# Three more row units in seven products, two of them worked in pairs; a norm's root as a power; another order in the last unit

## The chip, the cores and the metric

The kernel runs on one core of a Trainium2 chip. The metric is device time in microseconds (us), the median of three runs. Beside it stands one execution that the hardware profiler recorded; its views are what is quoted below. In them PE is TensorE's matmul, PEld its weight load, DVE is VectorE, ACT is ScalarE, POOL is GpSimd and SP is SyncE, which issues most DMAs. "L705" is a line of the kernel's source.

## The reference

One layer of a streaming encoder in fp32 on x of 1024 positions by 1024 channels; the feed-forward width is 3072:

```python
h = rms_norm(x, norm1_w)
q, k, v, g_ret, x_lru, y_lru, gate_ret, gate_lru = split(h @ w_in)       # 1024 x 7168
q, k = rotary(q), rotary(k) * dk**-0.5
o = chunkwise_retention(q, k, v)                   # 4 heads, chunks of 64
y_a = (head_group_norm(o, ret_gn_w) * silu(g_ret)) @ w_ret_o
hl = rg_lru(causal_conv(x_lru), ...)               # block-diagonal gates, scan over positions
y_b = (hl * gelu(y_lru)) @ w_lru_o
mix = sigmoid(gate_ret + b0) * y_a + sigmoid(gate_lru + b1) * y_b
x = x + mix @ w_out
h = rms_norm(x, norm2_w)
gate, val = split(h @ ffn_w_up)                    # 1024 x 6144
x = x + (gelu(causal_conv3(gate)) * val) @ ffn_w_down     # 3072 x 1024
return rms_norm(x, norm_f_w)
```

## The kernel before, in words

**Units.** Every large product is cut into *units* (class `Job`): a block of 256 output rows (two 128-row halves m) by 1024 positions (two 512-column halves) with 1024 inner channels (two halves k). The operand with the positions, four blocks B11, B12, B21, B22 of four 128x512 tiles each, stays in SBUF for all units of a product; the weights A11, A12, A21, A22 of each unit are loaded from DRAM. For fp32 accuracy each tile is split in a high and a low part (`split`: ACT casts at L424, DVE subtracts at L425), and each product of a weight tile with an operand tile is three matmuls 128x128 by 128x512 (`PASSES`).

**Eight or seven products.** One block product is 4 tiles x 3 passes = 12 matmuls. A *standard* unit makes 8 of them, 96 matmuls (`mm_std`, `mm_by` at L650, `mm_first` L681). A *fast* unit uses the scheme of Strassen and Winograd with 7, so 84 matmuls (`mm_fast`, L705). It takes sums of weight blocks (S1 = A21+A22, S2 = S1-A11, S3 = A21-A11, S4 = A12-S2, made by DVE at L510 to L526) against sums of operand blocks (T1 = B12-B11, T2 = B22-T1, T3 = B12-B22, T4 = B21-T2). Products and sets go together so: A11 with B11, S1 with T1, S2 with T2, A12 with B21, S3 with T3, A22 with T4, S4 with B22, in this order. The results gather in three PSUM banks X, Y and Z; ACT copies a bank out (`keep`, L719), DVE adds (`more` L725, `total` L729). The operand sets are made once for all units of a product by *builders* (`operand` loads blocks and splits them, `tsets` makes T1 to T4 tile by tile).

Standard before are the four units of the retention output, the first of LRU output, of FFN up and of FFN down, and the very first unit of all (the constants `FAST_RO`, `FAST_LO`, `STD_U` and `g + t` say which are fast).

**The order of the work.** The kernel body is Python that emits instructions while generators for weight loads (`loads`, L470), weight preparation (`preps`) and builders are advanced between products. It is built twice: class `Plan` reads the instructions of the first build with their dependencies, gives each a due time in a backward pass with costs set by hand, and lists them in a forward pass (`forward`): on each engine the most urgent ready instruction is next. The second build is held to that order on every engine, SP's queue of DMAs included.

**Places that the steps below speak of.** At the start `params` (128 rows of 200 columns of scales and biases) comes by one DMA on ACT's queue (L1462), the first x tile beside it (L1458); DVE then scales x tiles into high and low parts (L878 to L881, ACT's part of it at L880 and L893). The rotary turn swaps two halves of a tile by DMAs (L1175, L1176), multiplies and adds on DVE (L1177 to L1179) and transposes on PE (L1187). Gates are written to DRAM as they are finished (`sg_d`, L1305). After the output product the second RMSNorm turns positions into columns: statistics (L1547, L1548), root (`rstd_of`, L796 to L801, on ACT and DVE), scaling (L1569), PE transposes (L1577), evictions as high part, low part and plain copy (L1580 to L1582); L1115 is a PE product of the LRU gates. FFN down sums its parts in `down_sums`, the last unit ends with the final norm (squares at L1742, a power on POOL at L1746, scaling at L1753, output DMA).

Of the kernel before, what the change touches and what calls it, by code (L numbers as in the profile page):

```python
# [18 lines left out]
P = 128  # L19
D = 1024  # L20
T = 1024
KT = 8
# [176 lines left out]
class Plan:  # L199
# [6 lines left out]
    LATE_DMA, LATE_PE, BACKLOG, KEEP = 1500.0, 400.0, 300.0, 2000.0  # L206

# [12 lines left out]
    def __init__(self, steps, nc):  # L220
        self.steps = {s.name: s for s in steps if s.outs and s.eng in self.ENGINES}
        edges = {n: [a for a, _ in nc.dependency_edges(n, None)] for n in nc.inst_names()}
        self.before, self.after = {}, {n: [] for n in self.steps}
        for n in self.steps:
            found, todo, seen = [], [n], {n}
            while todo:
                for a in edges.get(todo.pop(), ()):
                    if a not in seen:
                        seen.add(a)
                        (found if a in self.steps else todo).append(a)  # L230
            self.before[n] = found
            for a in found:
                self.after[a].append(n)
# [60 lines left out]
    def forward(self, rank):  # L294
# [16 lines left out]
        for _ in range(len(self.steps)):  # L311
# [13 lines left out]
            if e == "Activation" and switch(item[1]) and item[0] > t + self.KEEP:  # L325
                item = min((q for q in ready[e] if not switch(q[1])), default=item)
            ready[e].remove(item)
# [6 lines left out]
            order[e].append(n)  # L334
            free[e] = t + s.hold
# [29 lines left out]
PASSES = ((0, 0), (0, 1), (1, 0))  # L365
NU = 81
# [18 lines left out]
def tile_trunk_layer(ctx, tc, x, xt, positions, params, consts, normf, w_in, w_ro, w_lo,  # L385
# [51 lines left out]
    class Job:  # L437
        def __init__(self, src, op, emit, post=None, fast=False, last=False, drop12=False,
                     pre=None, fetch=None, order=None, ready=None, by=None, rate=RATE):
            self.pre, self.ready, self.by, self.rate = pre, ready, by, rate  # L440
            self.order = order or (("A11", "A21", "A22", "A12") if fast else ORD_T)
# [17 lines left out]
    def loads():  # L459
        i = 0  # L460
        while True:
            while i >= len(queue):
                yield None
            jb = queue[i]
            for nm in jb.order:
                m, kh = int(nm[1]) - 1, int(nm[2]) - 1
                while jb.ready is not None and not jb.ready(m, kh):
                    yield None
                t = W.get()
                SY.dma_start(t, jb.src(m, kh))  # L470
                jb.raw[nm] = t
                state["raws"] += 1
                yield True
            i += 1
# [11 lines left out]

    def preps():
        i = 0
        while True:
            while i >= len(queue):  # L490
                yield None
            jb = queue[i]

            def fin(nm, src):
                jb.blk[nm] = split(src, W.get)
                state["blocks"] += 1

            if not jb.fast:
                for nm in jb.order:
                    fin(nm, (yield from raw(jb, nm)))  # L500
                    done(jb, nm)
                    yield True
            else:
                a11 = yield from raw(jb, "A11")
                fin("A11", a11)
                yield True
                a21 = yield from raw(jb, "A21")
                a22 = yield from raw(jb, "A22")
                s1 = W.get()
                V.tensor_add(s1, a21, a22)  # L510
                fin("S1", s1)
                yield True
                V.tensor_sub(s1, s1, a11)  # L513
                fin("S2", s1)
                yield True
                a12 = yield from raw(jb, "A12")
                fin("A12", a12)
                yield True
                V.tensor_sub(a11, a21, a11)  # L519
                fin("S3", a11)  # L520
                done(jb, "A11", "A21")
                yield True
                fin("A22", a22)
                done(jb, "A22")
                yield True
                V.tensor_sub(s1, a12, s1)  # L526
                fin("S4", s1)
                W.put(s1, late=SOONER)
                done(jb, "A12")
                yield True  # L530
            i += 1
# [163 lines left out]
    def mm_fast(jb, op):  # L695
        X, Y, Z = psg.get(), psg.get(), psg.get()

        def prod(bank, an, bn, first):
            pump((jb, an))
            w = jb.blk[an]  # L700
            n = 0
            for j in range(4):
                c = slice(128 * j, 128 * j + 128)
                for a, b in PASSES:
                    PE.matmul(bank, w[a][:, c], need(op, (bn, j))[b], start=first and n == 0, stop=n == 11,  # L705
# [4 lines left out]
            if jb.last:  # L710
                for j in range(4):
                    drop(op.pop((bn, j)))
            pump()
            build(BRATE)
            advance(RATE)

        def keep(bank):
            u = get()
            S.copy(u, bank)  # L719
            return u  # L720

        def more(u, m, c):
# [4 lines left out]

        def total(u, bank, m, c):
            V.tensor_add(u, bank, u)  # L729
            jb.emit(m, c, u, u)  # L730

        prod(X, "A11", "B11", True)
        s1 = keep(X)
        yield
        jb.ask(0, 0)
        prod(Z, "S1", "T1", True)
        prod(X, "S2", "T2", False)
        u2 = keep(X)
        more(s1, 0, 0)
        jb.ask(1, 1)  # L740
        prod(Y, "A12", "B21", True)
        total(s1, Y, 0, 0)
        psg.put(Y)
        jb.ask(1, 0)
        prod(X, "S3", "T3", False)
        u3 = keep(X)
        more(u3, 1, 1)
        total(u3, Z, 1, 1)
        yield
        jb.ask(0, 1)  # L750
        prod(X, "A22", "T4", False)
        jb.emit(1, 0, X, None)
        psg.put(X)
        more(u2, 0, 1)
        prod(Z, "S4", "B22", False)
        total(u2, Z, 0, 1)
        psg.put(Z)

    def run(jobs, between=None):
# [4 lines left out]
        ahead = None  # L764
        for jb, nx in zip(jobs, jobs[1:] + [None]):
            if jb.fast:
                g = ahead
                if g is None:
                    g = mm_fast(jb, jb.op)
# [3 lines left out]
                if nx is not None and nx.fast and nx.op is jb.op:  # L773
                    ahead = mm_fast(nx, nx.op)
# [8 lines left out]
            if jb.post is not None:  # L783
                g = jb.post()
                if g is not None:
                    back.append(g)
# [46 lines left out]
    def tsets(op, fetch, ahead=AHEAD_T, here=False):  # L833
        tiles = reads(fetch, [(n, j) for j in range(4) for n in ("B11", "B12", "B21", "B22")], ahead)
        for j in range(4):
# [16 lines left out]
            yield 2.4  # L852

# [579 lines left out]
    def u_start():  # L1433
        drain()
        builders.append(operand(u, from_dram(u_d), FAST_LO > 0))
# [11 lines left out]
    half = pool.tile([P, 1], F32, tag="half", name="half")  # L1447
# [14 lines left out]
    nc.scalar.dma_start(par, params)  # L1462
# [8 lines left out]
    for k in (2, 3):  # L1471
        xget(k, 0)
    next(state["load"])
# [70 lines left out]
    def out_post(t):  # L1544
        def fn():
# [3 lines left out]
            rstd_of(r, v, w)  # L1549
# [4 lines left out]
    def norm_half(half):  # L1554
# [18 lines left out]
        for k in range(KT):  # L1573
# [5 lines left out]
            hi, lo, f = get(F32R), get(F32R), get()  # L1579
            S.activation(hi, ps, AF.Copy, scale=w)  # L1580
            V.scalar_tensor_tensor(lo, ps, w, hi.bitcast(F32), ALU.mult, ALU.subtract)
            S.activation(f, ps, AF.Copy, scale=w)  # L1582
            h2[f"B{k // 4 + 1}{half + 1}", k % 4] = (hi, lo)
            keep2[f"B{k // 4 + 1}{half + 1}", k % 4] = f
# [261 lines left out]
```

## Time and profile before

| | before |
|---|---|
| median of three runs | 1614.21 us (1613.81 to 1616.84) |
| profiled execution, its own time | 1613.97 us |
| span of that execution | 1612.2 us |
| PE busy | 1599.3 us, 99% of the span |
| DVE, ACT, POOL busy | 1320.6 (82%), 908.2 (56%), 45.8 (3%) |
| matmul records of fast units (L705), of `mm_by` (L650) | 5544, 768 |
| DMA | 271.11 MB, 168 GB/s in the mean |

The span is what the records cover; the execution's own time is 1.8 us longer. Busy times are sums of the records of one engine; those of PE overlap, so its share says that it hardly stops, and the price of one matmul is read from a chain of many in a row. Where another engine or a DMA matters, it does so only at the few places at which PE waits.

### The profile page before, as it was taken

The page shows a single profiled execution, that of the slowest core. Times are in us where ns is not written, and L with a number is a line of the kernel's source. Part 1 is how long each engine was busy: PE and PEld are TensorE (multiplying, and loading weights), DVE is VectorE, ACT ScalarE, POOL GpSimd, SP SyncE. Part 2 cuts the span into 40 slices and gives each one's busy share as a digit, 9 for nine tenths or more (in the row PEclk, how much of TensorE's full clock was granted, in tenths as well). Part 3 has the DMA queues.
Part 4 walks back from the last instruction along what each step waited for, and adds up shares of the span by engine and source line. Part 5 has one row for each costly group of instructions (what it writes and reads, how often), then busy time and mean ns, then how long its engine had stood idle before and what let it go on. Part 6 is the DMA issues. An engine that isn't in the chain of part 4 may idle for free.

```text
span 1612.2 us, 21662 instructions
## 1 busy us (share of the span) xinstructions
PE 1599.3 (99%) x7176; PEld 1320.5 (82%) x7176; DVE 1320.6 (82%) x2393; ACT 908.2 (56%) x1534; POOL 45.8 (3%) x68
## 2 busy tenths in 40 slices
PE   9999999999999999999999999999999999999998
PEld 7887888888888888888888888888888888888886
DVE  8998768686898899968788799777777778888885
ACT  7475535444696878934364775444444446554553
POOL 0010000000000000000000001000000000000000
PEclk9999999999999999999999999999999999999999
DMA  8245324242242337775797236444444456878761
GB/s 298 66 133 162 118 72 138 66 131 85 92 144 95 128 93 267 236 261 201 228 333 248 99 124 199 142 131 137 137 133 144 135 189 217 285 241 277 256 217 66
DMA packets 151441, 271.11 MB, mean 168 GB/s; under 512 B 16800, under 2 KB 25120, under 8 KB 151328
## 3 DMA queue, kind: packets, MB, share of 16 engines
q1 hardware_dynamic: 145664, 253.63, 48.3%
q0 software_dynamic: 4224, 13.64, 2.7%
q10 hardware_dynamic: 1440, 2.46, 0.4%
q8 instruction: 56, 0.92, 0.2%
q14 instruction: 57, 0.47, 0.1%
HBM read 188.92 MB, written 75.50 MB: 164 GB/s over the span
## 4 chain that ended last, share of the span: by engine, by line
PE 61%; DVE 2%; ACT 2%; issue 1%; POOLq 0%; POOL 0%; DVEq 0%; ACTq 0%
PE g L705 50%; PE g L650 10%; DVE u L1097 1%; PE a L1115 1%; DVE u L425 0%; PE a L1577 0%; ACT u L1118 0%; DVE w L425 0%; ACT L1118 0%; ACT L1138 0%; DVE u L729 0%; ACT u L424 0%; ACT u L1126 0%; DVE u L1058 0%; ACT L1304 0%
## 5 line engine op out<-in xcount | busy, mean ns | idle before, releaser
L705 PE MATMUL g<-u,w 128*128 128x512 f32 x5544 | 1296.1, 392 | 0.7 <-ACT u L719 0.7
L705 PEld LDWEIGHTS g<-u,w 128*128 128x128 f32 x5544 | 1035.3, 188 | 212.2 <-ACT u L719 1.1
L424 ACT CAST w<-w 128x512 fp32r<-128x512 f32 x502 | 309.8, 621 | 405.0 <-PE g L705 280.6
L425 DVE TENSOR_TENSOR w<-w,w 128x512 fp32r<-128x512 f32 x502 | 342.0, 685 | 91.0 <-ACT w L424 86.8
L729 DVE TENSOR_TENSOR u<-g,u 128x512 f32<-128x512 f32 x198 | 135.7, 687 | 78.3 <-PE g L705 58.9
L650 PE MATMUL g<-u,w 128*128 128x512 f32 x768 | 179.6, 390 | 0.0
L424 ACT CAST u<-u 128x512 fp32r<-128x512 f32 x224 | 132.0, 620 | 70.4 <-PE g L705 12.4
L650 PEld LDWEIGHTS g<-u,w 128*128 128x128 f32 x768 | 143.7, 188 | 29.4
L719 ACT COPY u<-g 128x512 f32<-128x512 f32 x198 | 114.9, 580 | 76.4 <-PE g L705 74.9
L425 DVE TENSOR_TENSOR u<-u,u 128x512 fp32r<-128x512 f32 x224 | 146.5, 684 | 4.8 <-ACT u L424 4.5
L1623 DVE SCALAR_TENSOR_TENSOR u<-u,par,u 128x511 f32<-128x511 f32 (+1 forms) x96 | 71.4, 745 | 3.9 <-ACT u L1620 3.5
L1628 POOL DMA_DIRECT2D ff_d<-u x48 | 36.1, 752 | 1237.6 <-DVE u L1627 1237.6
L1115 PE MATMUL a<-u,u 128*128 128x512 f32 x192 | 50.4, 394 | 0.6 <-ACT u L424 0.4
L1620 ACT ACTIVATE u<-u,par 128x512 f32<-128x512 f32 x48 | 39.3, 818 | 15.4 <-DVE u L729 15.0
L513 DVE TENSOR_TENSOR w<-w,w 128x512 f32<-128x512 f32 x66 | 45.3, 687 | 1.2
L519 DVE TENSOR_TENSOR w<-w,w 128x512 f32<-128x512 f32 x66 | 45.3, 686 | 0.5
L526 DVE TENSOR_TENSOR w<-w,w 128x512 f32<-128x512 f32 x66 | 45.3, 686 | 0.4
L510 DVE TENSOR_TENSOR w<-w,w 128x512 f32<-128x512 f32 x66 | 45.2, 685 | 0.5 <-DMA w<-w_up 0.4
L725 DVE TENSOR_TENSOR u<-u,u 128x512 f32<-128x512 f32 x42 | 28.8, 687 | 19.9 <-ACT u L719 19.8
L1115 PEld LDWEIGHTS a<-u,u 128*128 128x128 f32 x192 | 35.2, 188 | 10.4 <-ACT u L424 1.8
L1627 DVE TENSOR_TENSOR u<-u,u 128x512 f32<-128x512 f32 x48 | 33.0, 687 | 5.8 <-ACT u L1626 5.7
L1097 DVE SCALAR_TENSOR_TENSOR u<-u,par,u 128x511 f32<-128x511 f32 (+2 forms) x48 | 35.4, 744 | 0.0
(189 smaller groups left out, 1123.4 us busy)
## 6 DMA issues: line engine op xcount, KB each, us to landing
w<-w_in SPq DMA_DIRECT2D x112, 256.0 KB, 2.7
w<-w_up SPq DMA_DIRECT2D x96, 256.0 KB, 2.7
u<-w_dn SPq DMA_DIRECT2D x88, 256.0 KB, 3.2
u<-x_d SPq DMA_DIRECT2D x60, 256.0 KB, 4.6
x_d<-u SPq DMA_DIRECT2D x48, 256.0 KB, 3.7
ff_d<-u POOLq DMA_DIRECT2D x48, 256.0 KB, 2.9
td_d<-u SPq DMA_DIRECT2D x48, 256.0 KB, 3.1
w<-ff_d SPq DMA_DIRECT2D x48, 256.0 KB, 3.7
```

The lines of the kernel that those rows point to most:

```text
L424: S.copy(hi, src)
L425: V.tensor_sub(lo, src, hi.bitcast(F32))
L513: V.tensor_sub(s1, s1, a11)
L519: V.tensor_sub(a11, a21, a11)
L526: V.tensor_sub(s1, a12, s1)
L650: PE.matmul(banks[m, h], jb.blk[an][a][:, c], o[b], start=left[m, h] == 2 and n == 0, stop=left[m, h] == 1 and n == 11)
L705: PE.matmul(bank, w[a][:, c], need(op, (bn, j))[b], start=first and n == 0, stop=n == 11, skip_group_check=True)
L719: S.copy(u, bank)
L729: V.tensor_add(u, bank, u)
L1097: V.scalar_tensor_tensor(c[:, s:], src[:, :TH - s], w, c[:, s:], ALU.mult, ALU.add)
L1115: PE.matmul(ps, wg[g][a][:, cs], xs[k][b], start=q == 0, stop=q == 5)
L1623: V.scalar_tensor_tensor(c[:, s:], src[:, :TH - s], w, c[:, s:], ALU.mult, ALU.add)
```

## The change

**More units in seven products.** The first unit of LRU output, of FFN up and of FFN down become fast, so only the first unit of all and the four of the retention output stay standard. To have enough PE work for each operand set while the sets are still being made, the first two units of LRU output and of FFN up are worked as a pair (`mate`): product by product, first for the one, then for the other unit, with six banks; loads and weight preparation alternate likewise.

**Order of products.** A fast unit may now have its own order (`prods`): the two first FFN-up units take `EARLY` (A11, A12, S4, S1, S2, S3, A22: the plain blocks B11, B21, B22 first, the T sets after), the last FFN-down unit takes `ENDING` (A12 later and S2 ahead of S1). Two new builders make sets in the order in which products take them: `seven` for the LRU operand and the first FFN-down group (four loads of each block instead of eight), `set_by_set` for FFN up.

```diff
+PRODS = ("A11", "S1", "S2", "A12", "S3", "A22", "S4")
+ENDING = ("A11", "S2", "S1", "S3", "A12", "A22", "S4")
+EARLY = ("A11", "A12", "S4", "S1", "S2", "S3", "A22")
+SETS = {"A11": "B11", "S1": "T1", "S2": "T2", "A12": "B21", "S3": "T3", "A22": "T4", "S4": "B22"}
+BANKS = {"A11": "X", "S1": "Z", "S2": "X", "A12": "Y", "S3": "X", "A22": "X", "S4": "Z"}
...
-    def mm_fast(jb, op):
-        X, Y, Z = psg.get(), psg.get(), psg.get()
+    def mm_fast(group, op):
...
+        for i, nm in enumerate(plan):
+            for jb in group:
...
+                prod(jb, bank, nm)
+                if nm in ("A11", "S2", "S3") or over and nm == "S4":
+                    u = kept[jb, nm] = get()
+                    S.copy(u, bank)
...
+    def set_by_set(op, b):
+        for j in range(4):
+            V.tensor_sub(b["B11", j], b["B12", j], b["B11", j])
+            op["T1", j] = split(b["B11", j])
+            yield 1.2
...
     def u_start():
         drain()
-        builders.append(operand(u, from_dram(u_d), FAST_LO > 0))
+        builders.append(seven(u, from_dram(u_d)))
...
-        ojobs.append(Job(pair_src(w_lo, n), u, emit_lru_o(n), fast=n >= 4 - FAST_LO, last=n == 3,
-                        drop12=n == 3 - FAST_LO, fetch=from_sg_t1(n),
-                         by=None if n >= 4 - FAST_LO else "k", order=None if n >= 4 - FAST_LO else BY_K))
+        ojobs.append(Job(pair_src(w_lo, n), u, emit_lru_o(n), fast=True, last=n == 3, mate=n == 0,
+                         fetch=from_sg_t1(n)))
...
-        if not g:
-            yield from operand(dop[g], fetch, False)
-            yield from kept_sums(dop[g], td_d[g])
-            return
...
+    ups = [Job(pair_src(w_up, i), h2, emit_to(gvs[i % 2]), up_post(i), fast=True, last=i == NF - 1,
+               mate=i == 0, prods=EARLY if i < 2 else PRODS,
+               order=("A11", "A12", "A21", "A22") if i < 2 else None) for i in range(NF)]
...
-                 emit_down(g, t, g + t > 0), down_post(g, t), fast=g + t > 0, last=t == 3, drop12=g + t == 0,
+                 emit_down(g, t, True), down_post(g, t), fast=True, last=t == 3,
+                 prods=ENDING if (g, t) == (2, 3) else PRODS,
                  pre=((0, 0), (0, 1), (1, 1)), fetch=from_x1(t),
-                 by=None if g + t else "k", order=None if g + t else BY_K,
```

**Second norm.** The root is one power on POOL, for two columns at a time. For the second half of the positions the transposed tiles come in the order 4 to 7, then 0 to 3, and B12, which no product takes as it stands, is no longer split. **Parameters** come as 8 columns first and the other 192 after four x tiles, on SP's queue.

```diff
-            rstd_of(r, v, w)
+            G.tensor_tensor(r, v, half, ALU.pow)
...
-        for k in range(KT):
+        for k in (range(KT), (4, 5, 6, 7, 0, 1, 2, 3))[half]:
...
-            builders.append(tsets(h2, lambda n, j: keep2[n, j], here=True))
+            builders.append(set_by_set(h2, keep2))
...
-    nc.scalar.dma_start(par, params)
+    nc.scalar.dma_start(par[:, 0:8], params[:, 0:8])
...
     for k in (2, 3):
         xget(k, 0)
+    SY.dma_start(par[:, 8:], params[:, 8:])
```

**The planner.** `Plan` now also counts who freed the buffer that a later instruction of the same tile writes, and in the forward pass DVE and ACT may stay idle for an instruction that will be ready within `NEAR` after the present one would end and is due more than `APART` (10,000 ns) earlier.

```diff
+    NEAR, APART = 500.0, 10000.0
...
+            if e in ("DVE", "Activation"):
+                soon = min(((rank[n], at) for at, n in wait[e] if at < t + self.steps[item[1]].hold + self.NEAR),
+                           default=None)
+                if soon and soon[0] < min(t, item[0] - self.APART):
+                    free[e] = soon[1]
+                    continue
```

What it does to the order of the instructions is shown at three places. The first is ACT's queue at the start, before; `par` is the tile of parameters, `w_27` and `w_30` are the high parts of the first two weight tiles, the `u` tiles are x and its scaled parts:

```order
L1458 DMA u_82_95<-xt 128x512
L1462 DMA par<-params 128x200
L1466 ACT_TABLE_LOAD
L1466 ACTIVATE st<-st 128x1
L893 ACTIVATE u_146_334<-u_82_95,par 128x512
L424 CAST w_27_151<-w_23_92 128x512
L424 CAST w_30_155<-w_24_99 128x512
L880 ACTIVATE u_100_159<-u_83_97,par 128x512
```

and now:

```order
L1577 DMA u_82_95<-xt 128x512
L1581 DMA par<-params 128x8
L1585 ACT_TABLE_LOAD
L1585 ACTIVATE st<-st 128x1
L451 CAST w_27_152<-w_23_92 128x512
L451 CAST w_30_156<-w_24_99 128x512
L1000 ACTIVATE u_100_160<-u_83_97,par 128x512
```

The scaling for the sums (L893) has moved behind both casts, and the load ahead of them is 8 columns wide. The second place is SP's queue at the second rotary turn, before. The DMAs from L1175 and L1176 swap halves of a tile, `sg_d` and `y_d` are finished gates written to DRAM, `w_in` is a weight load; `u_301` and `u_247` are the same buffer under two names:

```order
L1176 DMA u_308_1542<-u_298_1385 64x512
L1175 DMA u_308_1542<-u_298_1385 64x512
L1305 DMA sg_d<-u_247_821 128x512
L1176 DMA u_301_1471<-u_293_1267 64x512
L470 DMA w_250_1430<-w_in 128x512
L1305 DMA sg_d<-u_273_1036 128x512
L1073 DMA y_d<-u_279_1172 128x512
L1176 DMA u_306_1518<-u_300_1432 64x512
L1175 DMA u_306_1518<-u_300_1432 64x512
```

and now:

```order
L1296 DMA u_308_1543<-u_298_1386 64x512
L1295 DMA u_308_1543<-u_298_1386 64x512
L1425 DMA sg_d<-u_247_820 128x512
L1425 DMA sg_d<-u_273_1037 128x512
L500 DMA w_251_1433<-w_in 128x512
L500 DMA w_250_1429<-w_in 128x512
L1296 DMA u_306_1519<-u_300_1431 64x512
L1295 DMA u_306_1519<-u_300_1431 64x512
L1193 DMA y_d<-u_294_1287 128x512
L1193 DMA y_d<-u_279_1172 128x512
L1296 DMA u_301_1471<-u_293_1266 64x512
```

The swap into `u_301`, which must wait until `u_247` is written out, stood ahead of the swap into `u_306` and stands behind it now. The third place is PE's queue in the first FFN-up units, before. `g_268`, `g_267` and `g_271` are PSUM banks, the `w` tiles are weights:

```order
L650 MATMUL g_268_8981<-u_1682_8915,w_1442_8618 128x512
L650 MATMUL g_268_8981<-u_1683_8916,w_1442_8618 128x512
L650 MATMUL g_268_8981<-u_1682_8915,w_1443_8619 128x512
L705 MATMUL g_271_9095<-u_1593_8629,w_1448_8664 128x512
L650 MATMUL g_267_8957<-u_1685_8926,w_1436_8587 128x512
L650 MATMUL g_268_8981<-u_1685_8926,w_1442_8618 128x512
L705 MATMUL g_271_9095<-u_1594_8630,w_1448_8664 128x512
```

and now, where `g_267` and `g_268` are the Z banks of the first and the second unit, the `w_1483` and `w_1484` rows are S4 of the second, `w_1457`/`w_1458` S1 of the first and `w_1465` S1 of the second:

```order
L752 MATMUL g_268_8942<-u_1618_8819,w_1483_8893 128x512
L752 MATMUL g_268_8942<-u_1619_8820,w_1483_8893 128x512
L752 MATMUL g_268_8942<-u_1618_8819,w_1484_8894 128x512
L752 MATMUL g_267_8903<-u_1634_8926,w_1457_8605 128x512
L752 MATMUL g_267_8903<-u_1635_8927,w_1457_8605 128x512
L752 MATMUL g_267_8903<-u_1634_8926,w_1458_8606 128x512
L752 MATMUL g_267_8903<-u_1636_8931,w_1457_8605 128x512
L752 MATMUL g_268_8942<-u_1634_8926,w_1465_8694 128x512
L752 MATMUL g_268_8942<-u_1635_8927,w_1465_8694 128x512
```

Before, a standard unit's matmuls alternated with those of a fast one beside it; now S4 of the second unit ends on its Z bank, S1 of the first begins on the other, and four matmuls later S1 of the second writes the bank that S4 just left. Over the whole program PE has 36 matmuls of this size fewer (5796 from `mm_fast` and 480 from `mm_by`, against 5544 and 768), SP has 965 DMAs against 984, ACT 74 table loads against 75, and POOL 12 tensor operations against 8.

More of the change, by code (lines that the diff above doesn't have):

```diff
@@ L309, in switch @@
             return f in self.TABLES and table not in self.TABLES[f]
-        for _ in range(len(self.steps)):
+        left = len(self.steps)
+        while left:
             t, e = math.inf, None
@@ L491, in preps @@
                 yield None
[L492 to L531, printed above, removed]
+            group = queue[i:i + 1 + queue[i].mate]
+            todo = deque((prep_fast if jb.fast else prep_plain)(jb) for jb in group)
+            while todo:
+                got = next(todo[0], False)
+                if got is False:
+                    todo.popleft()
+                    continue
+                yield got
+                if got:
+                    todo.rotate(-1)
+            i += len(group)
     state["load"], state["prep"] = loads(), preps()
@@ L704, in prod @@
                 for a, b in PASSES:
-                    PE.matmul(bank, w[a][:, c], need(op, (bn, j))[b], start=first and n == 0, stop=n == 11,
+                    PE.matmul(bank, w[a][:, c], need(op, (SETS[nm], j))[b], start=first and n == 0, stop=n == 11,
                               skip_group_check=True)
@@ L763, in run @@
             pump()
-        ahead = None
-        for jb, nx in zip(jobs, jobs[1:] + [None]):
+        ahead, i = None, 0
+        while i < len(jobs):
+            jb = jobs[i]
+            group = jobs[i:i + 1 + jb.mate]
+            i += len(group)
+            nx = jobs[i] if i < len(jobs) else None
             if jb.fast:
```

259 lines of the change are left out of this document (188 added, 71 removed).

## The prediction

> **What bounds the kernel now.** I read the page's first part, then PE's own waits, then the chain that ended last, then the busy times by stage.
>
> ```profile
> PE 1599.3 (99%) x7176; PEld 1320.5 (82%) x7176; DVE 1320.6 (82%) x2393; ACT 908.2 (56%) x1534; POOL 45.8 (3%) x68
> PE a L1187 <- DVE u L1179: 1.7, 1, 1.7
> PE g L681 <- ACT w L424: 1.5, 1, 1.5
> PE a L1469 <- DVE heat L1449: 1.4, 1, 1.4
> PE g L705 <- ACT u L719: 0.7, 1, 0.7
> 935.70 431.80 PE g L705 x1905
> L705 PE MATMUL g<-u,w 128*128 128x512 f32 x5544 | 1296.1, 392 | 0.7 <-ACT u L719 0.7
> L650 PE MATMUL g<-u,w 128*128 128x512 f32 x768 | 179.6, 390 | 0.0
> 80.00:120.00 40.00, 40.00 (x178) 33.11 (x178) 40.00 (x73) 29.52 (x43) 3.22 (x6) 1.00 0.41 129
> 885.00:905.00 20.00, 20.00 (x100) 16.51 (x98) 14.35 (x31) 12.31 (x25) 0.00 (x0) 1.00 0.47 166
> 920.00:935.00 15.00, 15.00 (x80) 12.58 (x79) 13.20 (x21) 14.97 (x26) 0.79 (x1) 1.00 0.17 54
> 935.00:950.00 15.00, 15.00 (x68) 12.43 (x67) 15.00 (x26) 9.66 (x18) 0.00 (x0) 1.00 0.39 123
> 1367.00:1382.00 15.00, 15.00 (x68) 12.36 (x67) 15.00 (x26) 13.61 (x25) 0.76 (x1) 1.00 1.00 351
> 1382.00:1397.00 15.00, 15.00 (x68) 12.43 (x67) 13.59 (x24) 4.81 (x9) 1.50 (x2) 1.00 0.92 319
> ```
>
> TensorE is busy 99% of the span and all its recorded waits come to 5.3 us. The seventh number of the first group must not be taken for a price: 392 ns is the time of one matmul from issue to its modelled end, and they overlap. The chain row gives the price that counts: 1905 matmuls in 431.80 us, so one more or one less is 0.2267 us. The stage rows (PE busy, PEld, DVE, ACT, POOL, clock, DMA share, GB/s) show where something else is near its limit without stopping PE: DVE has no idle time in 80–120, 935–950 and 1367–1382, ACT none in 920–935, and in 1367–1382 the DMA engines are full. Those are the places at which a change could turn PE's lead into a wait.
>
> **The change part by part.** The sum is made against the profiled execution's own 1613.97 us; the median of the three runs, 1614.21, lies 0.24 above.
>
> *Fewer matmuls.* Three units (the first of LRU output, of FFN up and of FFN down) go from 8 products of 12 matmuls to 7. 3 x 12 = 36 matmuls fewer, 36 x 0.2267 = 8.16 us, and PE is the bound on both sides of each place, so all of it lies on the path: −8.2 us. On back-to-back matmuls the Trainium skill (TensorE: Matmul & The Clock Gate, Back-to-back issue gap) gives about 131 ns as the sustained spacing at 512 columns. By that the term would be 4.7 us; the trace differs, 0.2267 us over 1905 in a row, and the measurement decides.
>
> *The start.* Before, one load of 100 KB brings all parameters; now 8 columns come first, and the planner puts another activation behind the first casts.
>
> ```profile
> par<-params ACTq DMA_DIRECT2D x1, 100.0 KB, 4.6
> u<-xt ACTq DMA_DIRECT2D x1, 256.0 KB, 4.0
> DMA to landing us min/median/max: 3.8/4.9/5.4
> 0.74 0.41 ACTq L1458 DMA_DIRECT2D u<-xt  x1
> 1.18 0.45 ACTq L1462 DMA_DIRECT2D par<-params  x1
> 5.86 0.72 ACT L893 ACTIVATE u<-u,par 128x512 f32<-128x512 f32 x1 [2.70 <-DMA par<-params]
> 5.88 0.49 DVE L878 TENSOR_SCALAR u<-u,par 128x512 fp32r<-128x512 f32 x1 [4.57 <-DMA par<-params]
> 6.49 1.12 ACT L424 CAST w<-w 128x512 fp32r<-128x512 f32 x2
> 7.14 5.10 PE L681 MATMUL g<-u,w 128*128 128x512 f32 x20 [1.46 <-ACT w L424]
> ```
>
> The parameters landed at 1.18 + 4.6 = 5.78 us, DVE began at 5.88, ACT ran L893 and only then the cast for which PE waited until 7.14. The first x tile was there at 0.74 + 4.0 = 4.74, the first weight at about 0.74 + 3.8 = 4.5 (the third row is of the weight loads L470 up to 14 us). With the small load landing beside the x tile, DVE begins at about 4.9, one us earlier, and the cast no longer stands behind L893, so the first matmul comes at about 5.5, 1.6 us earlier; the following ones need DVE's second and third result, so the lead settles nearer to DVE's. It is worth what DVE gains, since DVE is full in 80–120: I take −1.2 us (bounds 0, if another landing decides, and −1.8).
>
> *The swap of the rotary halves.* The one wait of 1.7 us in PE's list is here:
>
> ```profile
> 128.38 0.56 SPq L1305 DMA_DIRECT2D sg_d<-u  x1
> 132.30 0.46 SPq L1176 DMA_DIRECT2D u<-u  x1
> 134.44 0.47 SPq L1176 DMA_DIRECT2D u<-u  x1
> 134.96 0.59 SPq L1175 DMA_DIRECT2D u<-u  x1
> SPq L1176 <- DMA sg_d<-u: 3.3, 1, 3.3
> 130.26 0.57 ACT L1063 COPY u<-g 128x512 f32<-128x512 f32 x1
> 138.56 0.69 DVE L1178 TENSOR_TENSOR u<-u,u 128x512 f32<-128x512 f32 x1 [2.02 <-DMA u<-u]
> 141.12 0.66 PE L1187 MATMUL a<-cst,u 128*128 128x128 f32 x4 [1.72 <-DVE u L1179]
> ```
>
> The source tile was copied by 130.83, but SP's queue stood 3.3 us behind a swap whose target tile was still being written out, so the two DMAs that matter left at 134.44 and 134.96, DVE waited for them until 138.56 and PE until 141.12. In the new SP order nothing that waits on such a write stands ahead of that pair (two weight loads and two writes of finished tiles do). It can leave at about 131 to 132, lands by the same 3.5 us (134.96 to 138.56) at about 135, and the second transpose, now 12 matmuls after the first in PE's order, finds its data. I take the whole wait: −1.7 us (bounds 0 and −1.7).
>
> *The last unit.* With A12 put between S3 and A22, bank X is copied while A12 runs on bank Y.
>
> ```profile
> 1598.76 0.58 ACT L719 COPY u<-g 128x512 f32<-128x512 f32 x1 [1.27 <-PE g L705]
> 1599.40 5.32 PEld L705 LDWEIGHTS g<-u,w 128*128 128x128 f32 x24 [1.10 <-ACT u L719]
> ```
>
> PE's 0.7 us there goes: −0.7 (0 to −0.8). What follows S4, the last product, is as before.
>
> *Norm by a power.* Two tiny operations, then one on POOL in place of a square root on ACT and five on DVE.
>
> ```profile
> 1604.30 0.55 POOL L1746 TENSOR_TENSOR nst<-nst,half 128x1 f32<-128x1 f32 x1 [13.94 <-DVE nst L1742]
> 1604.88 1.33 ACT L1753 ACTIVATE u<-u,nst 128x512 f32<-128x512 f32 x2 [0.92 <-POOL nst L1746]
> 914.40 0.20 ACT L796 ACTIVATE nst<-nst 128x2 f32<-128x2 f32 x1 [0.43 <-DVE nst L1548]
> 915.63 1.67 DVE L1569 TENSOR_SCALAR u<-u,nst 128x512 f32<-128x512 f32 x4
> ```
>
> The old way took 914.40 to 915.63, 1.2 us; the power takes 0.58 and a handover of about 0.15 each way, but DVE now fills the gap with other rows. PE has 26 matmuls to run meanwhile: 0 (bounds −0.3 and +0.5).
>
> *The FFN-up pair.* This is the tight place. From its second B22 tile to the last T4 tile DVE has 43 instructions in the new order, almost all of the kind below; PE has from the first S4 matmul to the first of T4 108 matmuls and 16 transposes.
>
> ```profile
> 938.10 2.49 DVE L425 TENSOR_TENSOR u<-u,u 128x512 fp32r<-128x512 f32 x4
> ```
>
> Four in a row take 0.602 us each (2.49 less the overlap of 0.08), so DVE needs 43 x 0.60 = 25.9 us; PE takes 108 x 0.2267 + 16 x 0.11 = 26.2 us, and needs the last tile only 9 matmuls later, 2 us. DVE thus just keeps up. One wait I do expect: the second unit's S4 bank is copied by ACT (0.58 us, the copy row above) while only 4 matmuls, 0.9 us, stand before PE writes that bank again, and ACT is full hereabouts. +0.6 us (bounds 0 and +3, the latter if DVE falls behind by five tiles).
>
> *The LRU pair.* Each set serves 24 matmuls, 5.4 us, against 8 to 12 DVE instructions of 0.60; its tiles are loaded during the retention output's four units, 16 loads instead of 32. Covered by 87 us of matmuls; 0 (up to +1 where that cover fails).
>
> *FFN down, first unit.* Seven sets must stand in 19 us instead of four in 22, with DVE at 15.00 of 15 and DMA at 1.00 just there. But its loads (28 instead of 32) stand in SP's order some 20 us of PE's work ahead of use, and the later groups already start this way without a wait in PE's list. 0 (up to +3).
>
> Sum: −8.2 −1.2 −1.7 −0.7 +0.6 = −11.2, so 1613.97 − 11.2 = 1602.8, and 0.24 more against the median: **1603.0 us**.
>
> **The rivals.** (1) *The small gains stay out*: the swap still lands late and the earlier start is eaten by DVE, which is full until 120. For it: one wait of 1.7 us came from a single late write. Against it: the order of SP. 1603.0 + 1.2 + 1.7 = 1605.9. (2) *POOL holds DVE up*: each power stops a DVE instruction for its 0.55 us; two of the four fall into the tight stretch, 1.1 us, so 1604.1. The trace shows no case, since at 1604.30 DVE had nothing to run. The Trainium skill (SBUF — State Buffer, Who interferes with whom) says that a DVE instruction with two SBUF inputs and a GpSimd one that reads SBUF exclude each other. No run so far shows it here. (3) *DVE falls behind where sets are due in half the time, and the kernel is slower*: if each tile's subtraction, cast and subtraction ran one after the other with ACT (0.69 + 0.62 + 0.69 = 2.0 us) rather than overlapped, the up pair's 16 T tiles would need 32 us for 23 and the down unit's 28 tiles at 1.31 us 37 for 28.5 with its lead: 9 + 8 = 17 us lost, 1603.0 + 17 = 1620. It decides against the change from 14.4 us over 44 tiles, 0.33 us lost on each. Against it: DVE's four in a row at 0.60 without a wait for ACT; for it: DVE and ACT both full there. A half of that gives 1611.5. (4) *The change does not do it*: 1614; the order shows 36 matmuls fewer, so hardly.
>
> **How the numbers follow.** Forecast 0.66, rival 1 0.17, rival 2 0.05, rival 3 by half 0.05 and whole 0.05, rival 4 0.02. Low end: the start at −1.8, no wait in the up pair and 1 us from reordering elsewhere, 1603.0 − 2.2 = 1600.8. High end: the gains of rival 1 out and 2.6 us of waits in the pairs, 1608.5; beyond it lie rival 3 and 4 and what the forecast's own scatter leaves. Within 0.2%, about 3.2 us, a measurement of this kernel can't tell from no change: faster means below 1611.0. That holds the forecast, rivals 1 and 2 and a part of rival 3's half, less a little for what I haven't seen: 0.90; same 0.04; slower 0.06.
>
> **What would show it.** The first matmul of data before 6 us; PE's list of waits without L1187's successor and without the copy at the end; 36 matmuls fewer at 0.2267; in the up pair one wait of PE for ACT's copy below 1 us, DVE without idle time there. Wrong it is if PE waits for DVE more than 3 us in one of the three first units, or if the span falls by less than 8.

## The result and the profile after

The changed kernel takes **1601.96 us** (median of four runs; 1601.60 to 1602.82), beside 1614.12 us of the kernel before (four runs) on the same chip: a ratio of 0.9922, 95% interval 0.9905 to 0.9939, so 12.2 us less. The forecast was 1603.0 in a range of 1600.8 to 1608.5. Runs at a slightly lower granted clock are longer: over the 43 runs of the kernel before that were taken beside the experiments, those at 0.999 of full clock took 1613.5 to 1615.2 us and those at 0.998 or 0.997 took 1614.4 to 1617.1, and three of the four runs of the first kernel with one more unit, at the end of the experiments, were at 0.998.

From the page of the changed kernel: the busy times, the two groups of product matmuls, and under them the whole list of PE's waits (us in total, times, longest) and the last piece of the chain that ended last.

```profile
PE 1591.4 (99%) x7140; PEld 1314.4 (82%) x7140; DVE 1326.9 (83%) x2393; ACT 910.3 (57%) x1534; POOL 49.5 (3%) x72
L752 PE MATMUL g<-u,w 128*128 128x512 f32 x5796 | 1353.9, 392 | 0.0
L691 PE MATMUL g<-u,w 128*128 128x512 f32 x480 | 110.8, 389 | 0.0
PE a L1588 <- DVE heat L1568: 1.4, 1, 1.4
PE g L722 <- DVE u L1001: 0.2, 1, 0.2
922.46 667.93 PE g L752 x2945
```

There are 36 matmuls fewer, at an unchanged price: 667.93 / 2945 = 0.2268 us. Of the five waits of before, the one for the warm-up tile (`heat`, 1.4 us, unchanged) and 0.2 us at the first product are left. From 922.46 us to the last product the chain is PE alone, but for two stops of 0.3 us together that are shown below. (The part on the kernel left out two standard units, which stay standard: the second unit of all, L610, and the first of the output product. The 768 matmuls from L650 are eight units, and 480 are five.)

Where the time went is read from instructions that both kernels have. The view of one line gives how often it ran, its durations, and its first and last start in us. First the first product, the products of the LRU gates and the transposes of the second norm before, then the same three after:

```profile
L681 PE MATMUL g<-u,w x96: 389/389/504, 7.1 to 29.1; 128*128 128x512 f32 x96
L1115 PE MATMUL a<-u,u x192: 387/389/501, 426.4 to 676.4; 128*128 128x512 f32 x192
L1577 PE MATMUL a<-cst,u x64: 270/272/275, 888.6 to 930.9; 128*128 128x128 f32 x64
```

```profile
L722 PE MATMUL g<-u,w x96: 387/389/500, 6.1 to 28.7; 128*128 128x512 f32 x96
L1235 PE MATMUL a<-u,u x192: 387/389/501, 424.5 to 672.0; 128*128 128x512 f32 x192
L1697 PE MATMUL a<-cst,u x64: 270/272/275, 882.6 to 922.2; 128*128 128x128 f32 x64
```

The new kernel is 0.4 us ahead at 29 us, 1.9 at the first LRU gate, and 6.0 at the first transpose of the norm. The first LRU unit accounts for 2.7 of the last step; 1.4 us more were gained between 426 and 889 us that no term of the forecast holds. From there to the end another 6.4 us come in the span (12.4 in all), of which two units are 5.4 and the wait in the last unit 0.95.

### The profile page after: what moved, and what is told of

Read it like the earlier page. It is cut to its first block, busy times and chain, and to the rows that moved or that the text cites. A ratio compares the mean times of both kernels' runs of the same rounds, so it can differ in the third digit from the quotient of the medians.

```text
span 1599.8 us, 21569 instructions
## 1 busy us (share of the span) xinstructions
PE 1591.4 (99%) x7140; PEld 1314.4 (82%) x7140; DVE 1326.9 (83%) x2393; ACT 910.3 (57%) x1534; POOL 49.5 (3%) x72
## 4 chain that ended last, share of the span: by engine, by line
PE 99%; DMA 0%; issue 0%; DVE 0%; ACT 0%; SPq 0%; POOLq 0%; POOL 0%; DVEq 0%; ACTq 0%
PE g L752 82%; PE g L691 7%; PE a L1235 3%; PE g L651 1%; PE g L722 1%; PE a L1346 1%; PE a L1348 1%; PE a L1357 1%; PE a L1341 0%; PE a L1407 0%; PE a L1697 0%; PE a L1324 0%; DMA u<-xt 0%; PE a L1307 0%; PE a L1052 0%
## 5 line engine op out<-in xcount | busy, mean ns | idle before, releaser
L451 ACT CAST w<-w 128x512 fp32r<-128x512 f32 x511 | 315.6, 622 | 401.4 <-PE g L752 274.7
L452 DVE TENSOR_TENSOR w<-w,w 128x512 fp32r<-128x512 f32 x511 | 348.6, 687 | 84.0 <-ACT w L451 77.6
L776 DVE TENSOR_TENSOR u<-g,u 128x512 f32<-128x512 f32 x207 | 142.2, 688 | 71.2 <-PE g L752 53.0
L791 ACT COPY u<-g 128x512 f32<-128x512 f32 x209 | 121.5, 582 | 91.1 <-PE g L752 89.0
L451 ACT CAST u<-u 128x512 fp32r<-128x512 f32 x216 | 126.6, 621 | 54.5 <-PE g L752 10.6
L452 DVE TENSOR_TENSOR u<-u,u 128x512 fp32r<-128x512 f32 x216 | 141.1, 687 | 5.0 <-PE g L691 3.1
L540 DVE TENSOR_TENSOR w<-w,w 128x512 f32<-128x512 f32 x69 | 47.4, 687 | 4.5 <-DMA w<-w_lo 4.1
L534 DVE TENSOR_TENSOR w<-w,w 128x512 f32<-128x512 f32 x69 | 47.4, 686 | 1.9 <-DMA w<-w_lo 1.9
L537 DVE TENSOR_TENSOR w<-w,w 128x512 f32<-128x512 f32 x69 | 47.5, 689 | 1.1
L543 DVE TENSOR_TENSOR w<-w,w 128x512 f32<-128x512 f32 x69 | 47.3, 686 | 0.4
```

Source lines behind the costliest of these rows:

```text
L451: S.copy(hi, src)
L452: V.tensor_sub(lo, src, hi.bitcast(F32))
L534: V.tensor_add(s, r["A21"], r["A22"])
L537: V.tensor_sub(s, s, r["A11"])
L540: V.tensor_sub(s, r["A12"], s)
L543: V.tensor_sub(src, r["A21"], r["A11"])
```

## Experiments

Medians of the runs scatter by some 0.3 us, those of the kernel before by more (1613.94, 1615.28, 1614.67 and 1614.05 at four times), and the ratio's interval is some 0.0016 to either side; so what is smaller than a microsecond is read from PE's records: the start of a matmul less that of the one ahead of it, over the usual 0.227 us.

**Each unit put back to eight products.** Three kernels, one edit each (the first shown; the others restore the deleted lines of the diff above for FFN up, with the split of B12 and the old order of the tiles, and for FFN down):

```diff
-        builders.append(seven(u, from_dram(u_d)))
+        builders.append(operand(u, from_dram(u_d), True))
...
-        ojobs.append(Job(pair_src(w_lo, n), u, emit_lru_o(n), fast=True, last=n == 3, mate=n == 0,
+        ojobs.append(Job(pair_src(w_lo, n), u, emit_lru_o(n), fast=n >= 4 - FAST_LO, last=n == 3,
```

> The changed kernel, with the first LRU-output unit in eight products again (its operand by the old builder, no pair). Theory (matmuls are the whole gain of a unit, 12 x 0.2267 = 2.72 us): 1602.0 + 2.7 = 1604.7, and no wait of PE comes or goes around 660 to 720 us. Rival (the pair lets work slip out of the full stretch before it, so that the gain is more than its matmuls): 1606 or more, with PE waits over 0.3 us at the LRU gates' products. Rival (the sets due in half the time take back a part): 1603.5 or less.

> The changed kernel, with the first FFN-up unit in eight products again (no pair, the T sets tile by tile, B12 split, all transposed tiles in the order 0 to 7). Theory: 12 matmuls more and no wait on either side, 1602.0 + 2.7 = 1604.7. Rival (the pair's S4 copy and the T sets take 0.6 us or more back from the gain): 1604.1 or less, and the small waits of PE between 920 and 930 us go. Rival (DVE falls behind in the pair): 1600 or less, excluded if the profile of the changed kernel is right that PE hardly waits.

> The changed kernel, with the first FFN-down unit in eight products again (four sets first, T sets after). Theory: 12 matmuls more and nothing else, 1602.0 + 2.7 = 1604.7. Rival (full DMA and DVE at 1355 to 1385 us cost something on one side): off from 1604.7 by over 1 us, with PE waits there.

Measured: 1604.40, 1604.46 and 1604.91 us, that is 2.4, 2.5 and 3.0 us above the changed kernel, 7.9 together where 36 matmuls are 8.2; with a scatter of 0.3 us each agrees with 2.7. PE's lists have no wait at 660 to 720 us or at 1355 to 1385 us in any of them, so the rivals of the first and the third fall. In the pair of FFN up one thing differs: with it PE stops twice more, for 0.19 and 0.11 us, behind the matmuls that start at 924.2 and 924.6; without it neither stop is there. The second rival is thus right about the stops, but they are 0.3 us and not 0.6. They stand where ACT copies the S4 bank, as this piece of ACT's timeline of the changed kernel shows (start, duration); PE goes on at 924.57, right behind the copy's end:

```profile
923.39 0.64 ACT L451 CAST u<-u 128x512 fp32r<-128x512 f32 x1
923.90 0.62 ACT L791 COPY u<-g 128x512 f32<-128x512 f32 x1
924.38 1.71 ACT L451 CAST u<-u 128x512 fp32r<-128x512 f32 x3
```

**The planner alone, and one of its two rules.** The kernel before with the new class `Plan`, then the same without the rule on staying idle, so that only the counting of freed buffers is new:

> The kernel before with the new planner alone: no unit, no set, no load and no norm is changed. Theory (the planner's rules are what took away the swap's wait, 1.8 us, and the waits at the LRU gates' products, 1.3 us): 1614.1 - 3.1 = 1611.0, PE waits for the first transpose of the second rotary turn and at the three gate products gone from the profile. Rival (these waits went because units, loads and the parameters' DMA moved): 1614.1 with both kept. In between (only the swap's): 1612.3.

> The kernel before with one of the planner's two rules alone: freed buffers count, DVE and ACT never stay idle for a later instruction. Theory (the write to DRAM that frees the swap's target gets an earlier due time, so the swap that stood in SP's queue is no longer held, wherever it stands): 1614.1 - 1.8 = 1612.3, no PE wait at the second rotary transposition, the three waits at the LRU gates' products as before. Rival (it took both rules): 1614.1 and the wait of 1.9 us stays. The start as before, first matmul after 7 us.

Measured: 1612.13 us (1612.01 to 1612.29) and 1612.57 us (1612.25 to 1613.11), beside 1613.94 and 1614.67 of before on the same chip at the time. In both the wait of 1.9 us at the second rotary transposition is gone; counting freed buffers does it alone. The three waits at the LRU gates stayed, in PE's list of the kernel with the planner alone:

```profile
PE a L1134 <- ACT u L443: 0.5, 2, 0.3
```

**The rule on idle time taken out of the changed kernel.**

> The changed kernel without the rule by which DVE and ACT may stay idle for a more urgent instruction. In SP's order the swap that waits for a write to DRAM stands ahead of the swap of the second transposition again, and on ACT the scaling for the sums ahead of the first cast. Theory (this one rule brought the gain at the swap and that at the start): PE waits 1.5 to 2 us at the second rotary transposition, the first matmul comes later than 6.1 us, and the time is 1602.0 + 1.8 + 0.4 = 1604.2. Rival (the smaller load of parameters brings the start, counting freed buffers the swap): 1602.0, and no such wait. The waits at the LRU gates' products stay away in both.

Measured: 1602.03 us (1601.83 to 1602.28). Theory and rival both fall in part. The swap that must wait for a write to DRAM stands ahead of the other one again, yet nothing waits. SP's timeline of this kernel:

```profile
124.15 0.94 SPq L1425 DMA_DIRECT2D sg_d<-u  x2
126.08 0.50 SPq L1296 DMA_DIRECT2D u<-u  x1
126.63 1.93 SPq L1295 DMA_DIRECT2D u<-u  x1
130.13 0.47 SPq L1296 DMA_DIRECT2D u<-u  x1
130.65 0.59 SPq L1295 DMA_DIRECT2D u<-u  x1
131.97 0.46 SPq L1296 DMA_DIRECT2D u<-u  x1
132.47 0.59 SPq L1295 DMA_DIRECT2D u<-u  x1
```

The write that frees the swap's target (first row) now leaves at 124.15, 6 us ahead of that swap (130.13), and lands 5.9 us after its issue, just in time; before it left at 128.38, directly ahead of the swap. SP's list of waits has none of a swap for this write. So the old order of the two swaps, on which the forecast rested this term, doesn't bring the wait back: it is enough that the write, with freed buffers counted, is due earlier. That isn't to say that the order does nothing in the changed kernel; there the write leaves at 127.75 only, as shown further down. The first matmul came at 7.19 us and not at 6.14, as the theory said, but without a price that the time could tell.

**Parameters in one load again.**

> The changed kernel with all parameters in one load again. Theory (a load of 4 KB lands no sooner than one of 100 KB, so the split is worth nothing): DVE's first instruction between 5.5 and 5.95 us as with the small load, 1602.0. Rival of the forecast (the small load brings DVE forward by a microsecond): 1603.0, with DVE's first instruction a microsecond later than 5.5.

Measured: 1602.24 us (1601.84 to 1602.60), DVE's first instruction at 5.58 us. (PE's list has one new row, two stops of 0.6 us together at the rotary transposes: every edit has the whole program planned anew.) The profiles of nine kernels, in us from the views of the parameter tile and the timelines (31st is the start of the 31st data matmul):

| kernel | load | landing after issue | DVE's first | first data matmul | 31st |
|---|---|---|---|---|---|
| before | 100 KB | 4.6 | 5.88 | 7.14 | 14.35 |
| planner alone | 100 KB | 4.6 | 5.93 | 6.56 | 14.38 |
| one rule alone | 100 KB | 4.4 | 5.66 | 6.92 | 14.13 |
| changed, one load | 100 KB | 4.3 | 5.58 | 6.22 | 14.03 |
| changed | 4 KB | 4.2 | 5.50 | 6.14 | 13.95 |
| LRU unit put back | 4 KB | 4.5 | 5.77 | 6.40 | 14.18 |
| idle rule out | 4 KB | 4.6 | 5.93 | 7.19 | 14.44 |
| LRU units unpaired | 4 KB | 4.1 | 5.39 | 6.02 | 13.80 |
| out_pair_early | 4 KB | 4.7 | 5.97 | 6.61 | 14.38 |

Small and large load land in the same span of time, 4.1 to 4.7 and 4.3 to 4.6; the other five kernels lie within it. The 31st matmul starts 8.4 to 8.5 us after DVE's first instruction in every row, whether the first matmul came early or late. So neither the split nor the earlier cast is worth anything; the 0.4 us by which the changed kernel's profile leads there is the scatter of one landing.

**All three units, the load, the root and the last unit as before.** What is left is the planner and the rewritten functions for loads, preparation and products:

```diff
+        builders.append(operand(u, from_dram(u_d), True))
...
+            rstd_of(r, v, w)
...
+    nc.scalar.dma_start(par, params)
```

> The changed kernel with all three units in eight products, the parameters in one load, the old root and the old order of the last unit: what is left of the change is the planner and the rewritten functions for products, loads and preparation, which take PSUM banks only when a product first needs one. Theory (these functions, not the units, took away PE's three waits at the LRU gates' products, 1.3 us that the planner alone left in): 1612.1 - 1.3 = 1610.8 and no PE wait over 0.2 us between 420 and 760 us. Rival (those waits went because of the parameters' load, the root or the units): 1612.1, with the three waits of 0.3 to 0.4 us as in the kernel with the planner alone.

Measured: 1610.73 us (1610.49 to 1611.53), 1.4 below the planner alone (on another chip), and PE's list of waits is empty between 400 and 700 us. So the rewritten functions, not the units, removed the waits at the LRU gates. Which of their parts did it, the banks that are taken when first needed or another, was not separated.

**The last unit in the usual order.**

```diff
-                 prods=ENDING if (g, t) == (2, 3) else PRODS,
+                 prods=PRODS,
```

> The changed kernel with the last unit in the usual order of products. Theory: PE's wait for the copy of bank X comes back with 0.84 + 0.11 us, 1602.0 + 0.95 = 1602.9, and everything ahead of the last unit is as in the changed kernel. Rival (the reordered unit only moves the wait, and the last evictions are what ends the span): 1602.0.

Measured: 1602.71 us (1602.55 to 1602.94). In PE's list, one row comes back, as before the change:

```profile
PE g L752 <- ACT u L791: 0.7, 1, 0.7
```

By the starts of matmuls it is 0.84 us, and 0.11 at the matmul after it.

**The LRU pair taken apart** (`mate=n == 0` removed):

> The changed kernel with the first two units of LRU output one after the other rather than as a pair; both in seven products, with the same builder. Theory (the operand's T sets stand at 722 us, some 23 us before the first product at 745 us, so that the pair is not what makes the gain there): 1602.0, no PE wait between 740 and 800 us. Rival (the sets, or the weights' sums of the first unit, are due in half the time and come late): PE waits of over 1 us in that stretch, 1603 or more.

Measured: 1602.11 us (1602.08 to 1602.33), no wait of PE there. The pair itself is worth nothing for this product; the sets stood long before.

**One more unit in seven products**, the first of the output product, with `FIRST` as its order and sets loaded in that order, once plainly and once with an earlier end of the LRU product:

```diff
+                 emit_out(t, True), out_post(t), fast=True, last=t == 3, mate=t == 0,
+                 prods=FIRST if t < 2 else PRODS, pre=((0, 0), (0, 1), (1, 1)), fetch=from_x(t),
+        builders.append(operand(wop, either, False, ("B11", "T3", "B21", "T1", "T2", "T4", "B22")))
```

> The changed kernel with the first unit of the output product, too, in seven products, in a pair with the second; order of products A11, S3, A12, S1, S2, A22, S4, since the first two need only the first half of the channels, and the sets are loaded in that order. Theory (a unit is worth its 12 matmuls where its sets can stand in time): 1602.0 - 2.7 = 1599.3. Rival (DMA is full between 800 and 840 us and the mixed rows come too late for products that need two blocks each): PE waits of 3 us or more between 820 and 850 us, 1602 or more.

> The output product's first two units as a pair in seven products, as in the run before, and the last LRU-output unit in the order A11, A12, S2, S3, A22, S1, S4: its two results in the first half of the positions are then complete 24 and 60 matmuls before its end (12 and 36 in the usual order), so the mixed rows for which the pair waited are written 12 matmuls, 2.7 us, earlier. Theory: of the 2.9 us wait 0.2 are left and 12 matmuls are saved, 1602.0 - 2.7 + 0.2 = 1599.5. Rival (what is late is not the mixed row but DMA or DVE, both full there): the wait stays above 2 us, 1602 or more.

Measured: 1604.63 us (1602.98 to 1604.88) and 1602.21 us (1601.82 to 1603.45); neither beats the changed kernel. The first kernel's 1602.98 is its profiled run, the one to set beside the others. PE's waits, in the first and in the second:

```profile
PE g L752 <- ACT w L451: 2.7, 1, 2.7
```

```profile
PE g L754 <- ACT w L453: 1.8, 1, 1.8
```

The 12 matmuls saved, 2.7 us, are paid back by this one wait: by the starts of matmuls it is 3.0 us in the first and 2.1 in the second. These are DVE, ACT and PE in the second kernel where the wait ends:

```profile
831.95 0.68 DVE L454 TENSOR_TENSOR u<-u,u 128x512 fp32r<-128x512 f32 x1
832.55 0.68 DVE L536 TENSOR_TENSOR w<-w,w 128x512 f32<-128x512 f32 x1
833.27 1.67 ACT L453 CAST w<-w 128x512 fp32r<-128x512 f32 x3 [0.54 <-DVE w L536]
833.94 0.73 PE L754 MATMUL g<-u,w 128*128 128x512 f32 x2 [1.84 <-ACT w L453]
```

The sum S1 of mixed rows comes at 832.55, right behind other DVE rows. Its load is the first of the three that leave SP from 826.46 on, and it lands 5.0 us after its issue, at about 831.5; so S1 stood 1.1 us in DVE's line, and before that it waited for the load. In the first kernel the same load left at 827.67. Moving the results 12 matmuls, 2.7 us, ahead thus moved the load by only 1.2 us, and took 0.9 off the wait. Why the load moved by so much less was not tried.

## Why the prediction was right

- **Fewer matmuls, −8.2.** Right, and shown: 7.9 us by putting each unit back, at an unchanged 0.2268 us a matmul. This is two thirds of the gain.
- **The start, −1.2.** This step failed. It let a 4 KB load land beside the x tile at 4.74, 3.6 us after its own issue, and let DVE begin at 4.9. The load landed after 4.2, as the large one does within its scatter, and DVE began at 5.50:

```profile
1.18 0.45 ACTq L1581 DMA_DIRECT2D par<-params  x1
4.36 0.62 ACT L451 CAST w<-w 128x512 fp32r<-128x512 f32 x1 [1.20 <-DMA w<-w_in]
5.50 0.49 DVE L998 TENSOR_SCALAR u<-u,par 128x512 fp32r<-128x512 f32 x1 [4.19 <-DMA par<-params]
6.14 0.47 PE L722 MATMUL g<-u,w 128*128 128x512 f32 x1
6.83 7.50 PE L722 MATMUL g<-u,w 128*128 128x512 f32 x30 [0.22 <-DVE u L1001]
```

  The cast did come off PE's path (4.36, not 6.49), but the first matmul came at 6.14 and not before 6. The step's own reservation, that the lead settles to what DVE gains, held: 0.4 us of it were left, by chance of the landing. The Trainium skill (DMA: Bandwidth & Descriptors, Anatomy of one DMA — SWDGE (gpsimd) path) gives, for DMAs that GpSimd issues, a fixed cost of about 2 us that doesn't grow with the size. This load was issued by ACT; that its size hardly counts up to 100 KB agrees with the table, but it takes 4.1 to 4.7 us, beside other loads in flight.
- **The swap, −1.7.** Right: the lead grows by 1.5 us from 29 to 426 us. The write, the pair of swaps that the second transposition needs, and the swap that needs the write leave SP like this in the changed kernel:

```profile
127.75 1.06 SPq L1425 DMA_DIRECT2D sg_d<-u  x2
130.63 0.47 SPq L1296 DMA_DIRECT2D u<-u  x1
131.15 0.59 SPq L1295 DMA_DIRECT2D u<-u  x1
132.93 0.48 SPq L1296 DMA_DIRECT2D u<-u  x1
```

  The pair leaves at 130.63 and 131.15, where the forecast said 131 to 132, and DVE takes its data at 135.14 without a wait, so PE goes on at 137.77 instead of 141.12:

```profile
135.14 0.69 DVE L1298 TENSOR_TENSOR u<-u,u 128x512 f32<-128x512 f32 x1
136.47 0.69 DVE L1299 TENSOR_TENSOR u<-u,u 128x512 f32<-128x512 f32 x1
137.77 0.60 PE L1307 MATMUL a<-cst,u 128*128 128x128 f32 x4
```

  The write (127.75, 4.2 us to land) would still have held a swap that stood ahead of the pair, so here the new order does what the forecast said. What the forecast didn't see is the rule behind it: counting freed buffers removes the wait alone, and it does so with the old order too, where it sends the write off at 124.15.
- **The last unit, −0.7.** Right, and a little low: the wait it removes is 0.84 + 0.11 us by the starts. The 0.7 of the list counts only from the modelled end of the matmul ahead, 0.39 us behind its start, where the next could have started 0.227 us behind it. The time without `ENDING` is 0.75 us longer.
- **The FFN-up pair, +0.6.** The wait for the copied S4 bank came where it was forecast, at half the size, 0.3 us by the starts. DVE kept up:

```profile
905.00:920.00 15.00, 15.00 (x79) 12.38 (x78) 14.43 (x26) 13.05 (x24) 1.06 (x1) 1.00 0.18 56
920.00:935.00 15.00, 15.00 (x72) 12.15 (x71) 14.67 (x25) 13.11 (x25) 0.00 (x0) 1.00 0.10 33
935.00:950.00 15.00, 15.00 (x68) 12.43 (x67) 15.00 (x26) 10.57 (x19) 0.00 (x0) 1.00 0.48 142
```

  DVE is at 14.43, 14.67 and 15.00 of 15 us, as near to its limit as the count of 43 instructions in 26 us said, and PE (second number) has no idle time in them. Rival 3, DVE falling behind, falls.
- **LRU pair and FFN down, 0.** Right. DVE is full at the start of FFN down (15.00 twice) and DMA at 1.00 in the first of these stretches, yet PE loses nothing:

```profile
1355.00:1370.00 15.00, 15.00 (x68) 12.43 (x67) 15.00 (x26) 14.37 (x28) 0.76 (x1) 1.00 1.00 369
1370.00:1385.00 15.00, 15.00 (x68) 12.43 (x67) 15.00 (x26) 7.80 (x14) 0.00 (x0) 1.00 0.75 242
```

- **What was missed, −1.4.** Three stops at the LRU gates' products, 0.30 to 0.41 us each by the starts before, each with 0.11 more at the next matmul. The forecast says nothing of them. Its list of PE's waits shows four of five rows, and its 5.3 us in all leave out the fifth:

```profile
PE a L1115 <- ACT u L424: 0.4, 2, 0.2
```

  The kernel without units, load, root and last order shows that the rewritten functions removed them.
- **The norm's power, 0, and rival 2.** The second norm's root was not tried by itself; with it PE has no wait in that stretch beyond those of the pair. On two columns it took 0.69 us at the least and up to 1.14, where the step had 0.58:

```profile
L1669 POOL TENSOR_TENSOR nst<-nst,half x4: 692/882/1139, 848.8 to 908.8; 128x2 f32<-128x2 f32 x4
```

Rival 1, that both small gains stay out, is half right: the start's did, the swap's did not. Put together, the parts as read above are 8.2 (matmuls), 0.4 (start, by chance), 1.5 (swap), 1.4 (LRU gates) and 0.95 (last unit), less 0.3 (FFN-up pair): about the 12.2 us that were measured. That the sum of 1603.0 came within 1.0 of the measurement is in part luck: the start fell 0.8 us short of its term, more than that came from the gates, which had none.

## What to carry to other kernels

In this kernel, where one engine is busy 99% of the span, work taken off it counted in full where a count of the instructions that feed it, at their pitch, fitted into the time it still needed; three units were worth what their matmuls cost. The fourth was not: its weight blocks are mixed rows that the work directly ahead of it writes, and the exposed chain of write, load, sum and cast cost about what the unit saved. SP's queue, issued in program order, was held for 3.3 us by a swap that waited for its buffer to be written out, so a planner should give the release of a buffer the urgency of its next use.

## What the runs showed of the hardware

A small operation on POOL that starts beside a running DVE instruction takes longer, and the next DVE instruction comes a little late. Of the changed kernel, the final norm's powers as a group (durations: least, median, longest), one that ran while DVE had nothing to do, and one beside DVE with the DVE rows around it:

```profile
L1865 POOL TENSOR_TENSOR nst<-nst,half x8: 539/545/995, 1538.2 to 1595.0; 128x1 f32<-128x1 f32 x8
1575.94 0.54 POOL L1865 TENSOR_TENSOR nst<-nst,half 128x1 f32<-128x1 f32 x1 [13.56 <-DVE nst L1861]
1541.37 0.99 POOL L1865 TENSOR_TENSOR nst<-nst,half 128x1 f32<-128x1 f32 x1 [2.62 <-DVE nst L1861]
1541.26 0.69 DVE L543 TENSOR_TENSOR w<-w,w 128x512 f32<-128x512 f32 x1
1541.97 0.69 DVE L452 TENSOR_TENSOR w<-w,w 128x512 fp32r<-128x512 f32 x1
```

The power took 0.99 us beside the running DVE instruction instead of 0.54, and DVE's next one started 0.71 us after it instead of the usual 0.60. Of the twelve powers of the changed kernel, the four that started less than 0.2 us behind a DVE instruction with two inputs in SBUF took 0.92 to 1.14 us, the eight others 0.54 to 0.70 (one column or two). So POOL, which came second, bore most of it, and DVE paid 0.1 us here, not the 0.55 of rival 2. The Trainium skill (SBUF — State Buffer, Who interferes with whom) says that a DVE instruction with two inputs in SBUF and a POOL one that reads SBUF exclude each other, and that the second one waits; for POOL as the second, these rows agree.
